# Zero-padded filter products, and a later inverse transform, in a one-core encoder trunk

## The chip, the cores and the metric

The program runs on one core of a Trainium2 chip. A core has a matmul engine (TensorE, PE in the profile, with its weight loads listed as PEld), a vector engine (VectorE, DVE), a scalar engine (ScalarE, ACT), GpSimd (POOL) and SyncE (SP), which here issues nearly all weight transfers. Each engine works through its own queue in order; they wait for one another through semaphores. The metric is the device time of one execution in microseconds (us), lower is better. The kernel before took 1728.81 us, the median of three runs (1728.32, 1728.81, 1731.26).

## The reference, cut to what matters

Two layers. Each has a hybrid token mixer (a short gated convolution and a Hyena operator, merged by gates) and then a channel mixer: a dense SwiGLU in layer 0, a top-2-of-8 expert SwiGLU in layer 1. One sequence of 256 positions, 1024 channels, float32. The change touches the Hyena part: its filters come out of a small network, and they are applied by Fourier transforms over all positions.

```python
def implicit_filters(L, w1, b1, freq, w2, b2, w3):
    z, t = hyena_pos_features(L)
    h = jnp.sin(fr * (z @ w1 + b1))
    h = jnp.sin(fr * (h @ w2 + b2))
    h = (h @ w3).reshape(L, N_DIRECTIONS, D_HYENA)          # the filter product
    h = h * decay_window(t)[:, None, :]
    h = h * lax.rsqrt(jnp.sum(jnp.square(h), axis=0, keepdims=True) + 1e-6)
    return h[:, 0], h[:, 1]

def bidirectional_fft_conv(u, k_fwd, k_bwd):
    kf = jnp.fft.rfft(kern, n=2 * L, axis=0)
    uf = jnp.fft.rfft(u, n=2 * L, axis=1)
    return jnp.fft.irfft(uf * kf[None], n=2 * L, axis=1)[:, :L]

    # in hybrid_mixer
    z = h_v * h_x1
    z = bidirectional_fft_conv(z, k_fwd, k_bwd) + z * hyena_bias
    y_h = h_x0 * z
    merged = g_a * (y_a @ w_a_out) + g_h * (y_h @ w_h_out)
    return merged @ w_o
```

## The kernel before, in words

**Number format.** TensorE multiplies in a reduced float32 form, so every operand is split into a high and a low part (`hilo`: ScalarE copies the high part, L167, VectorE subtracts it from the source, L168), and a product is made of three matmuls (`mm3`, L174 to L176). Weights arrive as chunks of 128x2048 floats (1 MB) in the buffers `wt`; each chunk is split in two halves, into six buffers `hl`, up to five halves ahead of their use.

**Chunks.** One projection of a 128x2048 weight chunk is 48 matmuls of 256 columns that accumulate into one of three PSUM banks called `mm`. In the mixer of either layer the order is: eight chunks for v and x1; then sixteen chunks, called here q0 to q15: four for x0, and twelve of the gated convolution, three for each quarter j. Of these three the first is copied out by ScalarE (L728), the second is multiplied by it on VectorE (L731, followed by the taps L583 and L585), the third is multiplied into the result by VectorE (L739) and split (`big`, L167 and L168). So q4, q7, q10 and q13 are of the first kind, q5, q8, q11 and q14 of the second, q6, q9, q12 and q15 of the third. Then come the sixteen chunks of the gate stage (per quarter: gate, `w_a_out`, gate, `w_h_out`), mixed with those of `w_o`. A bank `mm` is free again when the chunk three before has been taken out of it.

**The Fourier work** runs between the chunks, in two halves of the channels. `dft_a(half)` is 12 matmuls of 512 columns into four banks `acc`, and VectorE and ScalarE evict them (L660 to L662). `dft_b(half, q)` is the product with the filter's spectrum: four VectorE products (L672 to L675) and two on GpSimd (L676, L677). `dft_c(half)` is four GpSimd sums (L686, L687), each split into `yh` and `yl` by ScalarE and VectorE. `idft(half)` is the inverse transform: eight groups of four matmuls (L705 to L708), evicted by VectorE (L711, L714), multiplied by x0 on GpSimd (L717) and split. Its result is wanted by the first `w_h_out` chunk, the fourth chunk of the gate stage. Which of these steps follows which chunk stands in a table, `after`, which begins at chunk `o` and lists one entry per chunk:

```python
        o = 5 if l == 0 else 1
        for q, ev in enumerate(([(dft_a, 0)], [(dft_b, 0, 0)], [(dft_b, 0, 1)], [(dft_a, 1), (dft_c, 0)], [(dft_b, 1, 0)],
                                [(dft_b, 1, 1), (idft, 0)], [], [(dft_c, 1)], [], [(idft, 1)])):
```

So in layer 0 `dft_a(0)` follows q5 and `idft(1)` follows q14; in layer 1 they follow q1 and q10. The table gives the program order; a scheduler then sets the order of each engine's queue from it.

**The filters.** `flt_c(l, ct)`, eight for each layer, is a filter product: for each of two directions, one matmul of the network's output `fr` (128 rows: the high part of the 64 hidden units, twice) with the weights `wr` (64 rows high part, 64 rows low part), L405, and one of `fl` (64 rows: the low part) with the upper half of `wr`, L406. Layer 0's filters run between its own chunks (into banks `acc`); those of layer 1 run in layer 0's gate stage (four), between layer 0's mixer and its FFN (two) and in the FFN (two), into banks `mm`.

**Later stages.** After layer 1's mixer all the mixer's buffers become weight buffers (`W.extend`), and the expert stage streams its weights through them. Already in layer 1's gate stage three of the large buffers `big` are turned into weight buffers; SyncE fills them as soon as what used them is done.

Of the kernel before, what the change touches and what calls it, by code (L numbers as in the profile page):

```python
# [9 lines left out]
F32 = mybir.dt.float32  # L10
F32R = mybir.dt.float32r
BF16 = mybir.dt.bfloat16
I32 = mybir.dt.int32
U32 = mybir.dt.uint32
AF = mybir.ActivationFunctionType
ALU = mybir.AluOpType

P = 128
S = 256
# [194 lines left out]
def body(tc, nc, x, vec, rows, fg, winT, zT, fw1, fw2, fb, fw3, w_in, w_ao, w_ho, w_o, w13, w2,  # L214
         m13, m2, cst, out, dbg=None):
# [36 lines left out]
    xp = mix.enter_context(tc.tile_pool(name="xp", bufs=1))  # L252
    tmp = mix.enter_context(tc.tile_pool(name="tmp", bufs=10))

    def big8(shape, dt=F32):
        t = big.tile(list(shape), dt, name="big", tag="big")
        return t

    def t2k(shape=(P, 2, 256), dt=F32):
        t = tmp.tile(list(shape), dt, name="t2k", tag="t2k")  # L260
        return t
# [72 lines left out]
    W.load(3)  # L334
    ff = xp.tile([P, 2, 4, P], F32R)
    gg = xp.tile([P, 4, 2, P], F32R)
    fg_raw = big8([P, 2, 4, P])
    nc.sync.dma_start(fg_raw, fg)


    def sin_of(ps, l):

        b, which, n = ps[1], ps[2], ps[3]
        a = t2k([n, 256])
        nc.vector.tensor_scalar(out=a, in0=ps[0], scalar1=fb_s[:n, l, which:which + 1],
                                scalar2=fb_s[:n, l, 1:2], op0=ALU.add, op1=ALU.mult)
        q = t2k([n, 256])
        nc.vector.tensor_scalar(out=q, in0=a, scalar1=1.0 / TWO_PI, scalar2=MAGIC, op0=ALU.mult, op1=ALU.add)
        nc.vector.tensor_scalar(out=q, in0=q, scalar1=-MAGIC, scalar2=None, op0=ALU.add)
        for c in (C1, C2, C3):  # L350
            nc.vector.scalar_tensor_tensor(out=a, in0=q, scalar=-c, in1=a, op0=ALU.mult, op1=ALU.add)
        last["sin"] = nc.vector.tensor_scalar(out=a, in0=a, scalar1=-PI_F, scalar2=PI_F, op0=ALU.max, op1=ALU.min)
        last["sina"] = nc.scalar.activation(b, a, AF.Sin)
# [3 lines left out]
    def flt_bank(l, shape=(P, 2, 256)):  # L357
        return acc_bank(shape) if l == 0 else mm_bank(shape)

    def flt_h(l, which):  # L360

        n = 64 * (1 + which)
        if which == 0:
            flt_load(l, 0)
            flt_load(l, 1)
            lhs, rhs = fw1_s[:, l], zT_s
        else:
            lhs, rhs = fw2_s[:, l], fs.pop((l, "h"))
        ps = flt_bank(l, [n, S])
        nc.tensor.matmul(ps, lhs, rhs, start=True, stop=True)  # L370
        t = xp.tile([n, S], F32, name="fh", tag="fh")
        sin_of((ps, t, 2 * which, n), l)
        if which == 0:
            fs[l, "h"] = t
        else:
            fs[l] = xp.tile([P, S], F32R, name="fr", tag="fr"), xp.tile([64, S], F32R, name="fl", tag="fl")
            nc.scalar.activation(fs[l][0], t, AF.Copy)
            nc.vector.tensor_tensor(out=fs[l][1], in0=t[:64], in1=fs[l][0][:64].bitcast(F32), op=ALU.subtract)

    def flt_load(l, ct):  # L380
        if ct < 8:
            wn = tmp.tile([P, S], F32, name="wn", tag="wn", bufs=3)
            nc.sync.dma_start(wn, winT[ct])
            w3 = tmp.tile([P, 2, P], F32, name="w3", tag="w3", bufs=2)
            nc.sync.dma_start(w3, fw3[l, ct])
            fs[l, "w", ct] = wn, w3

    def flt_w(l, ct):

        if (l, "w", ct) in fs:  # L390
            wn, w3 = fs.pop((l, "w", ct))
            wr = tmp.tile([P, 2, P], F32R, name="wr", tag="wr", bufs=2)
            with tc.issue_after(last["sina"].ins):
                nc.scalar.activation(wr, w3, AF.Copy)
            nc.vector.tensor_tensor(out=wr[64:], in0=w3[64:], in1=wr[64:].bitcast(F32), op=ALU.subtract)
            fs[l, "p", ct] = wn, wr
            flt_load(l, ct + 2)

    def flt_c(l, ct):

        flt_w(l, ct)
        wn, wr = fs.pop((l, "p", ct))
        ps = flt_bank(l)
        for s in range(2):
            nc.tensor.matmul(ps[:, s], wr[:, s], fs[l][0], start=True, stop=False)  # L405
            nc.tensor.matmul(ps[:, s], wr[:64, s], fs[l][1], start=False, stop=True)  # L406
        if ct != 4 or l == 0:
            flt_w(l, ct + 1)
        hw = t2k()
        nc.vector.tensor_tensor(out=hw, in0=ps, in1=wn[:, None, :].to_broadcast([P, 2, S]), op=ALU.mult)  # L410
        ss = small.tile([P, 2], F32, name="ss", tag="ss")
        sd = t2k()
        for s in range(2):
            nc.scalar.activation(sd[:, s], hw[:, s], AF.Square, accum_out=ss[:, s:s + 1])
        rn = small.tile([P, 2], F32, name="rn", tag="rn")
        nc.gpsimd.tensor_scalar(out=rn, in0=ss, scalar1=1e-6, scalar2=None, op0=ALU.add)
        nc.gpsimd.tensor_tensor(out=rn, in0=rn, in1=mhalf, op=ALU.pow)
        for s in range(2):
            nc.scalar.activation(hw[:, s], hw[:, s], AF.Copy, scale=rn[:, s:s + 1])
        nc.gpsimd.memset(hw[:, 1, 0:1], 0.0)  # L420
        for s, op in enumerate((ALU.add, ALU.subtract)):
            nc.gpsimd.tensor_tensor(out=sd[:, s], in0=hw[:, 0], in1=hw[:, 1], op=op)
        fs[l, "sd", ct] = sd
# [44 lines left out]
    fs = {}  # L468
# [104 lines left out]
    def proj(parts, xs):  # L573

        xh, xl = xs
        ps = mm_bank()
        for pt in range(2):
            for k in range(KT):
                mm3(nc, ps[:, pt], parts(pt * D + k * P, P), (xh(k), xl(k)), k == 0, k == KT - 1)
        return ps  # L580
# [20 lines left out]
    def mixer(l, xh, xl):  # L601
# [21 lines left out]
        for j in range(4):  # L623
            ps = proj(W.next(), xs)
# [7 lines left out]
            ps = proj(W.next(), xs)  # L632
# [111 lines left out]

        sts = [{} for _ in range(4)]
        chunks = [(x0_chunk, j) for j in range(4)] + [(a_chunk, j, w, sts[j]) for j, w in A_ORDER]
        o = 5 if l == 0 else 1
        after = {1: [(z_parts, 3)]}
        for q, ev in enumerate(([(dft_a, 0)], [(dft_b, 0, 0)], [(dft_b, 0, 1)], [(dft_a, 1), (dft_c, 0)], [(dft_b, 1, 0)],
                                [(dft_b, 1, 1), (idft, 0)], [], [(dft_c, 1)], [], [(idft, 1)])):  # L750
            after[o + q] = after.get(o + q, []) + ev
        for q, (f, *a) in enumerate(chunks):
            f(*a)
# [16 lines left out]
        if l == 0:  # L770
            with W.behind():
                nc.scalar.activation(tri_b, tri_s, AF.Copy)
            steps.extend([[(flt_h, 1, 0)], [], [(flt_h, 1, 1)], [], [(flt_c, 1, 0)], [(flt_c, 1, 1)]]
                         + [[(flt_t, 1, c - 2), (flt_c, 1, c)] for c in (2, 3)] + [[(flt_t, 1, 2)], [(flt_t, 1, 3), (flt_w, 1, 5)]])

        for j in range(4):
            ps = proj(W.next(), xs)
# [3 lines left out]
            ps = proj(W.next(), yas)  # L781
            nc.vector.tensor_tensor(out=ga, in0=ps, in1=ga, op=ALU.mult)
            fill0()
            ps = proj(W.next(), xs)
# [3 lines left out]
            ps = proj(W.next(), yhs)  # L788
# [54 lines left out]
    with W.behind():  # L843
        flt_h(0, 0)
    W.after = (last["sin"].ins,)
    steps.extend([[], [], [(flt_h, 0, 1)], [(flt_c, 0, 0)], [(flt_c, 0, 1)]])
    for c in range(2, 8):
        steps.append([(flt_t, 0, c - 2), (flt_c, 0, c)] + ([(flt_d, 0, c // 2 - 2)] if c in (4, 6) else []))
# [4 lines left out]
    li = 0  # L853
    for l in range(DEPTH):
        acc = mixer(l, xh, xl)
        li += 1
        if l == 1:
# [373 lines left out]
    for r, v in enumerate(nc.values_load_multi_w_load_instructions(ix[0:1], engines=[mybir.EngineType.SP], min_val=0,  # L1231
# [4 lines left out]
                            in1=keys[:, None, :].to_broadcast([P, NE, NE]), op=ALU.is_equal)  # L1236
# [155 lines left out]
```

## Time and profile before

| | |
|---|---|
| median of three runs | 1728.81 us |
| the profiled execution, whole | 1726.32 us |
| its span in the profile | 1724.4 us |
| PE busy (share of the span) | 1670.5 us (97%) |
| DVE busy | 710.5 us (41%) |
| ACT busy | 491.7 us (29%) |
| POOL busy | 180.3 us (10%) |
| mean granted clock of TensorE | 0.982 |

The shares are means over unlike stages. In the page's picture of 40 slices (43.1 us each) VectorE is at 80 to 90% in most of the slices that hold layer 0's mixer (the first six), at about half in the FFN, high again in layer 1's mixer, and at 10 to 20% in the expert stage, which is over half of the span and runs at 90% or more on PE and on the DMA engines. A busy PE is no measure of its speed, as matmuls overlap: the distance from one start to the next is, and that is read from the timeline. What it waits for is in the list of waits.

### The profile page before, as it was taken

The page shows a single profiled execution, that of the slowest core. Times are in us where ns is not written, and L with a number is a line of the kernel's source. Part 1 is how long each engine was busy: PE and PEld are TensorE (multiplying, and loading weights), DVE is VectorE, ACT ScalarE, POOL GpSimd, SP SyncE. Part 2 cuts the span into 40 slices and gives each one's busy share as a digit, 9 for nine tenths or more (in the row PEclk, how much of TensorE's full clock was granted, in tenths as well). Part 3 has the DMA queues.
Part 4 walks back from the last instruction along what each step waited for, and adds up shares of the span by engine and source line. Part 5 has one row for each costly group of instructions (what it writes and reads, how often), then busy time and mean ns, then how long its engine had stood idle before and what let it go on. Part 6 is the DMA issues. An engine that isn't in the chain of part 4 may idle for free. (4 is left out here: it accounts for less than half of the span.)

```text
span 1724.4 us, 32503 instructions
## 1 busy us (share of the span) xinstructions
PE 1670.5 (97%) x14105; PEld 1091.8 (63%) x14105; DVE 710.5 (41%) x1009; ACT 491.7 (29%) x775; POOL 180.3 (10%) x163
## 2 busy tenths in 40 slices
PE   7999899899998999999999999999999999999996
PEld 6999899799997999999534333343343333434322
DVE  8989865765557899655410110101101011010112
ACT  4763565454543554543110100000001010010110
POOL 3424311210102034000110000000000000000000
PEclk9999999999998999999999999999999999999998
DMA  7443355355452543656698999999999999999993
GB/s 280 161 165 120 144 192 208 122 176 193 173 195 100 194 147 142 250 174 245 248 396 347 399 419 419 420 418 418 368 415 419 419 419 419 373 367 373 418 420 135
DMA packets 73580, 491.91 MB, mean 285 GB/s; under 512 B 8278, under 2 KB 13144, under 8 KB 14808
## 3 DMA queue, kind: packets, MB, share of 16 engines
q1 hardware_dynamic: 73000, 486.63, 71.7%
q0 software_dynamic: 432, 3.15, 0.5%
q8 instruction: 112, 1.84, 0.4%
q14 instruction: 36, 0.29, 0.0%
HBM read 488.70 MB, written 1.05 MB: 284 GB/s over the span
## 5 line engine op out<-in xcount | busy, mean ns | idle before, releaser
L1047 PE MATMUL mm<-wt,xe 128*32 128x512 f32 (+1 forms) x3664 | 473.5, 542 | 0.0
L176 PE MATMUL mm<-xh,hl 128*128 128x256 f32 x1376 | 393.0, 286 | 5.9 <-DVE hl L168 5.9
L174 PE MATMUL mm<-xh,hl 128*128 128x256 f32 x1376 | 394.4, 287 | 2.0 <-ACT xh L167 1.1
L175 PE MATMUL mm<-xl,hl 128*128 128x256 f32 x1376 | 393.2, 286 | 2.9 <-DVE xl L168 2.7
L168 DVE TENSOR_TENSOR hl<-wt,hl 128x1024 fp32r<-128x1024 f32 x234 | 305.7, 1311 | 145.2 <-ACT hl L167 144.4
L1047 PE MATMUL mm<-big,xe 128*32 128x512 f32 (+1 forms) x1712 | 295.9, 535 | 0.0
L167 ACT ACTIVATE hl<-wt 128x1024 fp32r<-128x1024 f32 x234 | 245.1, 1054 | 172.5 <-PE mm L176 97.4
L1047 PEld LDWEIGHTS mm<-wt,xe 128*32 128x32 f32 x3664 | 155.7, 110 | 210.9 <-issue 189.9
L176 PEld LDWEIGHTS mm<-xh,hl 128*128 128x128 f32 x1376 | 267.4, 194 | 6.4 <-DVE hl L168 6.3
L174 PEld LDWEIGHTS mm<-xh,hl 128*128 128x128 f32 x1376 | 267.6, 195 | 5.4 <-ACT xh L167 1.9
L175 PEld LDWEIGHTS mm<-xl,hl 128*128 128x128 f32 x1376 | 267.1, 194 | 4.9 <-DVE xl L168 3.9
L1057 DVE TENSOR_TENSOR act<-mm,act 128x512 f32<-128x512 f32 (+1 forms) x32 | 20.0, 625 | 483.4 <-PE mm L1047 483.4
L1096 PE MATMUL acc<-wt,at 128*32 128x512 f32 x1232 | 192.8, 593 | 0.0
L1047 PEld LDWEIGHTS mm<-big,xe 128*32 128x32 f32 x1712 | 86.4, 110 | 101.9 <-issue 91.4
L1056 ACT ACTIVATE act<-mm 128x512 f32<-128x512 f32 (+1 forms) x32 | 17.4, 544 | 457.0 <-PE mm L1047 457.0
L490 POOL TENSOR_TENSOR rs<-rs,mhalf 128x1 f32<-128x1 f32 x10 | 6.8, 675 | 1076.9 <-DVE rs L489 1076.9
L1096 PEld LDWEIGHTS acc<-wt,at 128*32 128x32 f32 x1232 | 53.1, 110 | 83.7 <-issue 82.9
L1096 PE MATMUL acc<-big,at 128*32 128x512 f32 x544 | 101.3, 593 | 0.0
L1101 PE MATMUL acc<-wt,bt 128*32 128x512 f32 x352 | 100.2, 592 | 0.0
L174 PE MATMUL mm<-big,hl 128*128 128x256 f32 x256 | 72.5, 283 | 0.0
L176 PE MATMUL mm<-big,hl 128*128 128x256 f32 x256 | 72.3, 282 | 0.0
L175 PE MATMUL mm<-big,hl 128*128 128x256 f32 x256 | 72.2, 282 | 0.0
(249 smaller groups left out, 1811.3 us busy)
## 6 DMA issues: line engine op xcount, KB each, us to landing
wt<-in_m_dram SPq DMA_DIRECT2D x231, 1024.0 KB, 12.6
big<-in_m_dram SPq DMA_DIRECT2D x103, 1024.0 KB, 13.3
wt<-in_w_in_dram SPq DMA_DIRECT2D x62, 1024.0 KB, 4.8
wt<-in_w_dram SPq DMA_DIRECT2D x33, 1024.0 KB, 4.9
wt<-in_w_ho_dram SPq DMA_DIRECT2D x8, 1024.0 KB, 5.7
wt<-in_w_ao_dram SPq DMA_DIRECT2D x7, 1024.0 KB, 4.8
wt<-in_w_o_dram SPq DMA_DIRECT2D x6, 1024.0 KB, 4.9
big<-in_rows_dram POOLq DMA_DIRECT2D x3, 1024.0 KB, 7.7
```

The lines of the kernel that those rows point to most:

```text
L167: a = nc.scalar.activation(hi, src, AF.Copy)
L168: v = nc.vector.tensor_tensor(out=lo, in0=src, in1=hi.bitcast(F32), op=ALU.subtract)
L174: nc.tensor.matmul(out, ah, bh, start=start, stop=False)
L175: nc.tensor.matmul(out, ah, bl, start=False, stop=False)
L176: nc.tensor.matmul(out, al, bh, start=False, stop=stop)
L490: last["pow"] = nc.gpsimd.tensor_tensor(out=rs, in0=rs, in1=mhalf[:, 0:1], op=ALU.pow)
L1047: nc.tensor.matmul(banks[r][32 * q:32 * q + 32, :n], xe[:, k, 32 * sg:32 * sg + 32], cols(w, b, q4), start=k == 0, stop=k == KT - 1, tile_ ...
L1056: nc.scalar.activation(a[:, :n], banks[0][:, :n], AF.Silu)
L1057: nc.vector.tensor_tensor(out=a[:, :n], in0=banks[1][:, :n], in1=a[:, :n], op=ALU.mult)
L1096: nc.tensor.matmul(ya[32 * q:32 * q + 32], at[:, f, 64 * b + 32 * sg:64 * b + 32 * sg + 32], ch[b][0][:, h * D + db * 512:h * D + (db + 1) ...
L1101: nc.tensor.matmul(yb[32 * q:32 * q + 32], bt[:, f, 32 * b:32 * b + 32], ch[b][0][:, h * D + db * 512:h * D + (db + 1) * 512], start=first ...
```

## The change

The low part `fl` is now one tile of 128 rows, made once and shared by both layers; its lower 64 rows are set to zero at the start by VectorE, and the second matmul of a filter product takes all 128 rows of `wr`. In the table, layer 0 begins one chunk earlier, and `idft(1)` stands two entries further back: in layer 0 all Fourier steps but `idft(1)` come one chunk earlier, and `idft(1)` one chunk later, after q15; in layer 1 `idft(1)` comes two chunks later, after q12, and nothing else moves.

```diff
+    fl = xp.tile([P, S], F32R)
+    nc.vector.memset(fl[64:].bitcast(U32), 0)
...
-            fs[l] = xp.tile([P, S], F32R, name="fr", tag="fr"), xp.tile([64, S], F32R, name="fl", tag="fl")
+            fs[l] = xp.tile([P, S], F32R, name="fr", tag="fr"), fl
             nc.scalar.activation(fs[l][0], t, AF.Copy)
-            nc.vector.tensor_tensor(out=fs[l][1], in0=t[:64], in1=fs[l][0][:64].bitcast(F32), op=ALU.subtract)
+            nc.vector.tensor_tensor(out=fl[:64], in0=t[:64], in1=fs[l][0][:64].bitcast(F32), op=ALU.subtract)
...
             nc.tensor.matmul(ps[:, s], wr[:, s], fs[l][0], start=True, stop=False)
-            nc.tensor.matmul(ps[:, s], wr[:64, s], fs[l][1], start=False, stop=True)
+            nc.tensor.matmul(ps[:, s], wr[:, s], fs[l][1], start=False, stop=True)
...
-        o = 5 if l == 0 else 1
+        o = 4 if l == 0 else 1
...
-                                [(dft_b, 1, 1), (idft, 0)], [], [(dft_c, 1)], [], [(idft, 1)])):
+                                [(dft_b, 1, 1), (idft, 0)], [], [(dft_c, 1)], [], [], [], [(idft, 1)])):
```

Lines after the new tile have a number higher by three in the changed kernel (L739 is L742 there). The scheduler's order moves with the table. VectorE's queue in layer 0, around q5 (whose product is L731): before, the eviction of `dft_a(0)` (L661, L662) stands behind that of q5 and of the last filter step (L460, L461).

```order
L168 TENSOR_TENSOR big<-acc,big 128x4x128
L168 TENSOR_TENSOR hl<-wt,hl 128x1024 x2
L731 TENSOR_TENSOR t2k<-mm,t2k 128x512
L168 TENSOR_TENSOR hl<-wt,hl 128x1024
L583 SCALAR_TENSOR_TENSOR t2k<-t2k,vec_s 128x255 x2
L585 SCALAR_TENSOR_TENSOR t2k<-t2k,vec_s 128x255 x2
L460 TENSOR_TENSOR big<-acc,t2k 128x256
L461 TENSOR_TENSOR big<-t2k,acc 128x256
L460 TENSOR_TENSOR big<-acc,t2k 128x256
L461 TENSOR_TENSOR big<-t2k,acc 128x256
L661 TENSOR_TENSOR t2k<-acc,t2k 128x512 x2
L662 TENSOR_TENSOR t2k<-t2k,acc 128x512 x2
```

Now, the same place of the same queue:

```order
L168 TENSOR_TENSOR big<-acc,big 128x4x128
L168 TENSOR_TENSOR hl<-wt,hl 128x1024
L664 TENSOR_TENSOR t2k<-acc,t2k 128x512 x2
L665 TENSOR_TENSOR t2k<-t2k,acc 128x512 x2
L168 TENSOR_TENSOR hl<-wt,hl 128x1024
L734 TENSOR_TENSOR t2k<-mm,t2k 128x512
L168 TENSOR_TENSOR hl<-wt,hl 128x1024
```

The eviction of `dft_a(0)` has moved ahead of q5's and of one weight split. VectorE's queue in layer 0 between the eviction of q11 (L731) and what follows that of q12 (L739), before:

```order
L731 TENSOR_TENSOR t2k<-mm,t2k 128x512
L168 TENSOR_TENSOR hl<-wt,hl 128x1024
L583 SCALAR_TENSOR_TENSOR t2k<-t2k,vec_s 128x255 x2
L585 SCALAR_TENSOR_TENSOR t2k<-t2k,vec_s 128x255 x2
L168 TENSOR_TENSOR hl<-wt,hl 128x1024
L739 TENSOR_TENSOR t2k<-mm,t2k 128x512
L168 TENSOR_TENSOR hl<-wt,hl 128x1024
L168 TENSOR_TENSOR big<-t2k,big 128x512 x5
```

And now:

```order
L734 TENSOR_TENSOR t2k<-mm,t2k 128x512
L168 TENSOR_TENSOR hl<-wt,hl 128x1024
L586 SCALAR_TENSOR_TENSOR t2k<-t2k,vec_s 128x255 x2
L588 SCALAR_TENSOR_TENSOR t2k<-t2k,vec_s 128x255 x2
L168 TENSOR_TENSOR big<-t2k,big 128x512 x4
L168 TENSOR_TENSOR hl<-wt,hl 128x1024
L742 TENSOR_TENSOR t2k<-mm,t2k 128x512
L168 TENSOR_TENSOR hl<-wt,hl 128x1024
```

The four splits of `dft_c(1)`, which `idft(1)` reads, have moved ahead of q12's eviction; the fifth `big` is q12's own. VectorE's queue in layer 1 from the eviction of q9 (L739) on, before; L711 and L714 are evictions of `idft(1)`, L731 that of q11:

```order
L739 TENSOR_TENSOR t2k<-mm,t2k 128x512
L168 TENSOR_TENSOR hl<-wt,hl 128x1024
L168 TENSOR_TENSOR big<-t2k,big 128x512
L168 TENSOR_TENSOR hl<-wt,hl 128x1024
L711 SCALAR_TENSOR_TENSOR t2k<-big,vec_s,acc 128x2x128
L168 TENSOR_TENSOR hl<-wt,hl 128x1024
L714 TENSOR_TENSOR t2k<-acc,t2k 128x2x128
```

And now:

```order
L742 TENSOR_TENSOR t2k<-mm,t2k 128x512
L168 TENSOR_TENSOR hl<-wt,hl 128x1024
L168 TENSOR_TENSOR big<-t2k,big 128x512
L168 TENSOR_TENSOR hl<-wt,hl 128x1024 x3
L734 TENSOR_TENSOR t2k<-mm,t2k 128x512
L168 TENSOR_TENSOR hl<-wt,hl 128x1024
L586 SCALAR_TENSOR_TENSOR t2k<-t2k,vec_s 128x255 x2
L588 SCALAR_TENSOR_TENSOR t2k<-t2k,vec_s 128x255 x2
```

Up to the third row the two queues are the same; behind it the evictions of `idft(1)` have gone back behind those of q11 and q12. Over the whole program VectorE's queue holds one instruction more than before, the zeroing; the other engines have the same instructions, and GpSimd also the same order.

## Rows read from the trace of the kernel before

**Rows 1.** Timeline, PE, one filter product (start us, duration us, engine, line, operation).

```profile
63.03 0.36 PE L405 MATMUL acc<-fr,wr 128*128 128x256 f32 x1
63.33 0.38 PE L406 MATMUL acc<-fl,wr 64*128 64x256 f32 x1
...
64.49 0.28 PE L175 MATMUL mm<-xl,hl 128*128 128x256 f32 x1
```

**Rows 2.** Timeline, PE, layer 0 from q14 to the gate stage (idle before, releaser).

```profile
183.30 0.36 PE L174 MATMUL mm<-xh,hl 128*128 128x256 f32 x1 [0.95 <-DVE t2k L731]
...
189.00 0.28 PE L176 MATMUL mm<-xh,hl 128*128 128x256 f32 x1
191.46 0.38 PE L705 MATMUL acc<-gg,big 128*128 128x256 f32 x1 [2.18 <-ACT big L167]
...
200.06 0.28 PE L174 MATMUL mm<-xh,hl 128*128 128x256 f32 x1
...
205.81 0.28 PE L174 MATMUL mm<-xh,hl 128*128 128x256 f32 x1
```

**Rows 3.** Timeline, PE, layer 1 from the end of q10 to q13.

```profile
674.91 0.28 PE L176 MATMUL mm<-xh,hl 128*128 128x256 f32 x1
675.88 0.39 PE L705 MATMUL acc<-gg,big 128*128 128x256 f32 x1 [0.69 <-ACT big L167]
...
684.83 0.28 PE L705 MATMUL acc<-gg,big 128*128 128x256 f32 x1
...
685.29 0.28 PE L174 MATMUL mm<-xh,hl 128*128 128x256 f32 x1
...
696.79 0.28 PE L174 MATMUL mm<-xh,hl 128*128 128x256 f32 x1
```

**Rows 4.** Stretches: length; busy us (instructions) by engine; PEclk, DMA share, GB/s.

```profile
57.00:121.00 64.00, 64.00 (x495) 60.77 (x496) 54.50 (x88) 46.55 (x104) 28.29 (x42) 1.00 0.49 166
121.31:190.16 68.85, 67.02 (x535) 65.44 (x533) 65.11 (x79) 27.12 (x38) 30.25 (x18) 1.00 0.35 123
192.90:199.70 6.80, 5.94 (x28) 5.94 (x29) 6.80 (x9) 5.25 (x8) 0.00 (x0) 0.50 0.58 226
677.60:684.40 6.80, 5.44 (x24) 5.25 (x25) 6.80 (x9) 4.26 (x6) 0.00 (x0) 0.50 0.42 157
840.00:860.00 20.00, 20.00 (x179) 9.34 (x180) 7.12 (x46) 2.10 (x4) 0.92 (x2) 1.00 0.20 67
860.00:1700.00 840.00, 831.97 (x7954) 317.48 (x7946) 82.79 (x146) 71.96 (x137) 5.52 (x2) 1.00 0.97 399
```

**Rows 5.** Tile fl: matmuls, duration ns min/median/max, first and last start.

```profile
L406 PE MATMUL acc<-fl,wr x16: 379/382/382, 54.8 to 105.2; 64*128 64x256 f32 x16
...
L406 PE MATMUL mm<-fl,wr x16: 379/382/579, 242.1 to 467.2; 64*128 64x256 f32 x16
```

**Rows 6.** Timeline, PEld, layer 0's second filter product.

```profile
55.88 0.19 PEld L405 LDWEIGHTS acc<-fr,wr 128*128 128x128 f32 x1 [0.24 <-DVE wr L395]
```

**Rows 7.** Timeline, PE, the first FFN chunk of layer 0.

```profile
343.44 0.41 PE L174 MATMUL mm<-xh,hl 128*128 128x256 f32 x1
343.98 0.58 PE L175 MATMUL mm<-xl,hl 128*128 128x256 f32 x1
```

**Rows 8.** Timeline, DVE: start of the program; layer 0; layer 1.

```profile
3.44 0.69 DVE L485 BATCH_NORM_STATS2 st<-big 128x6 f32<-128x512 f32 x1 [2.43 <-DMA big<-in_x_dram]
...
191.22 3.09 DVE L168 TENSOR_TENSOR big<-t2k,big 128x512 fp32r<-128x512 f32 x5
...
207.80 0.69 DVE L168 TENSOR_TENSOR big<-t2k,big 128x512 fp32r<-128x512 f32 x1 [2.13 <-ACT big L167]
...
681.04 0.68 DVE L739 TENSOR_TENSOR t2k<-mm,t2k 128x512 f32<-128x512 f32 x1
```

**Rows 9.** Timeline, POOL and SP, layer 1: last of idft(1), and a large buffer's transfer.

```profile
690.68 1.29 POOL L717 TENSOR_TENSOR t2k<-t2k,big 128x512 f32<-128x512 f32 x1 [1.87 <-DVE t2k L714]
...
706.00 0.38 SPq L99 DMA_DIRECT2D big<-in_w_ao_dram  x1
```

## The prediction

> **What bounds the kernel now.** I read the list of TensorE's waits first, then its timeline where it waits, then VectorE's queue beside it, and the stretches last. Two places stand out, one in each layer, and they are the same step: `idft(1)`. In layer 0 its first matmul starts at 191.46, 2.18 us of idling after q14's last one, and the step reaches to 200.06 [rows 2]; in layer 1 it reaches from 674.91 + 0.12 to 685.29 [rows 3]. Without a halt the eight groups take 8 x 0.46 = 3.7 us, by the last group of layer 1 (684.83 to 685.29) [rows 3]. Two things stretch it. It waits for the high and low parts of `dft_c(1)`, which stand late in the queues of ScalarE and VectorE. And right after these waits the granted clock is 0.50 for 6.8 us, in both layers [rows 4]: 1.2 GHz instead of 2.4, so the rest of the step runs at half speed. The third place is smaller but comes often: the filter products. Four of their matmuls and the one behind them take 63.03 to 64.49 = 1.46 us [rows 1], while a chunk's matmuls of the same 256 columns follow each other at (205.81 - 200.06) / 48 = 0.12 us [rows 2]. Every step into or out of a 64-row matmul costs 0.3 us from start to start; durations do not show this, because matmuls overlap.
>
> Behind TensorE stands VectorE. From 121.31 to 190.16 it is busy 65.11 of 68.85 us [rows 4]. So what TensorE is spared in layer 0 must be checked against VectorE's queue, not only against its own.
>
> The expert stage, more than half of the span, runs its DMA engines at a share of 0.97 [rows 4]. It passes an earlier start on in full, by this reading: between 840 and 860 the share is 0.20, since all buffers are already full, so the stream is tied to the buffers that the mixer's end hands over, and these come earlier by what the mixer saves.
>
> **The filter products.** Five starts at 0.12 instead of 1.46 us save 1.46 - 0.60 = 0.86 us a product, if 128 rows throughout remove the 0.3 us steps. There are 16 products (32 matmuls with `fl`, two each) [rows 5]. Not all lie on TensorE's path. Layer 0's first is followed at once by the second, which waits for its weights until 55.88 [rows 6], so the first gives nothing. The two between mixer and FFN are followed by a chunk that has to halt at its fifth start or so for the low part of the input (a step of 0.54 us at 343.98 where the half clock's step is 0.21) [rows 7]; they give nothing either. That leaves 7 in layer 0's chunks, 4 in the gate stage and 2 in the FFN. In the last two places TensorE waits for nobody, and I take the saving in full: 4 x 0.86 = 3.4 and 2 x 0.86 = 1.7 us.
>
> In layer 0 the seven are worth 6.0 us to TensorE. VectorE must follow; from 57 to 121 it is busy 54.50 of 64 us [rows 4], so it has 9.5 us of idle time, most of it spent waiting for ScalarE, whose work here follows TensorE's. I take 5.0 of the 6.0 us; the ends are 0 and 6.0. A loss is excluded, since 128-row matmuls cost 0.12 us everywhere else. The zeroing at the start costs nothing: VectorE idles 2.43 us there until x lands [rows 8]; without that cover it would be under 0.7 us, the row next to it.
>
> The Trainium skill speaks against all of this: its page TensorE: Matmul & The Clock Gate (Why this matters for your kernels) holds that one matmul on few rows takes the same time as one on 128, so that 64 more rows change nothing; by it this part is worth 0. Another page of the Trainium skill, TensorEngine Tiling (Array Packing), Key Properties, says that a change of tiling mode drains the engine; by it the part is worth what I have set. The trace leans to the second: 0.30 us from L405 to L406 [rows 1].
>
> **`idft(1)` in layer 1.** Nothing before q10's end moves, so the old times hold up to there: 675.03. Now q11 follows at once and ends at 675.03 + 5.75 = 680.8. q12 needs the bank of q9, which VectorE takes out at 681.04 + 0.68 = 681.7 [rows 8]; its queue is the same up to there, so q12 begins at 681.8, 1.0 us late, and ends at 687.5. By then the parts of `dft_c(1)` are long split, since the old step was through by 685.29. `idft(1)` takes 3.7 us without a halt, and q13 starts at 691.2 instead of 696.79 [rows 3]: 5.6 us. The ends are 685.29 - 675.03 - 3.7 = 6.6 (no wait at q12) and 3 (a halt for the second half's weights or a slower clock behind the wait). Halts of 0.95 us are no cause for the half clock here: after that at 183.30 in layer 0 the 48 matmuls took 189.12 - 183.30 = 5.8 us [rows 2].
>
> What is queued behind `idft(1)` moves with it. GpSimd's last product of it ends now at 690.68 + 1.29 = 692.0, and SyncE fills the third of the freed large buffers at 706.00 [rows 9]. Moved to 691.2 + 7 = 698, that product still ends before 706.00, so the weight queue is not held up.
>
> **The table in layer 0.** TensorE by itself would be spared the 0.95 us before q14 and the excess of `idft(1)`, 200.06 - 189.12 - 3.7 = 7.2: 8.2 us. VectorE gives less. The last thing that q15 waits for is the eviction of q12 (L739, L742 now), as q15 takes q12's bank. In the old order that eviction ends at 190.16, and from 121.31 to there VectorE has 65.11 us of work [rows 4]. The new order has the same instructions in front of it and, as the second pair of queue pieces shows, four splits more: 4/5 of 3.09 = 2.5 us [rows 8]. Run without a gap that is 121.31 + 67.6 = 188.9; with some 0.4 us at the start for `dft_a(0)`'s copies, 189.3. Then q15 (5.75) and `idft(1)` (3.7), which finds its inputs split before q15 began: the gate stage starts at 198.7 instead of 205.81 [rows 2], 7.1 us. If VectorE comes 5.0 us earlier through the filter products, both add: 12.1 us. TensorE's own bound then is 8.2 + 6.0 = 14.2 us, so VectorE sets the pace. Ends: 14.2, and 3.7, where VectorE gains nothing and one more halt brings 6.8 us at half speed as above, which costs 3.4 us. The result of `idft(1)` is late by nothing: before, its last split ends at 208.5 [rows 8], 8.4 us after the step; the first `w_h_out` chunk comes three chunks, 17 us, after it. Some 4 us more of queue stand before those evictions now, and it still fits.
>
> **The sum**, against the profiled execution of 1726.3 us: 7.1 + 5.0 + 3.4 + 1.7 + 5.6 = 22.8, so 1703.5. That execution lies 2.5 us under the median of the runs, which I add: 1706.0 us, or 1.3% faster.
>
> **Rivals.**
>
> *Rows do not matter.* The 0.3 us steps come from something else than 64 rows, such as one bank written twice in a row, and stay. For it: the two matmuls of a pair do share bank and weights. Against: the three matmuls of every split product share a bank too, and follow at 0.12. Then the filter terms go and the table's stay: 7.1 + 5.6 = 12.7, so 1716.1 us.
>
> *VectorE takes it back.* In layer 0 it is full, the earlier Fourier steps only push it into saturation sooner, it does not come forward at all, and TensorE's halts gather into one that again brings the half clock: 3.7 instead of 12.1 us, in all 14.4, so 1714.4 us. For it: 65.11 of 68.85 us. Against: 9.5 idle us ahead of that stretch.
>
> *Half clock for a long stretch, slower.* From q8 to q15 of layer 0 TensorE now waits a little at each chunk for VectorE, and the clock does not come back between. Each chunk then costs 5.75 us more; from five such chunks on the gain is eaten and the kernel is slower, and all eight would give about 1706 + 46 = 1752 us. For it: both halts before brought 0.50. Against: it came back after 6.8 us each time, and by the walk above TensorE halts once, at q15, for 1 to 2 us.
>
> *The weight stream does not start earlier.* If the expert stage is timed by something that the mixer does not move, the end stays at 1728.8 us. Against: the 0.20 between 840 and 860.
>
> **How the numbers follow.** Chances: the forecast 0.74, rows do not matter 0.09, VectorE takes it back 0.11, the long half clock 0.03, the stream 0.03. The low end is everything at its best: 14.2 + 3.4 + 1.7 + 6.6 and 1.6 for the two products between the stages, 27.5, so 1701.3; the runs shown scatter by 2 to 3 us, so 1699. The upper end has to hold the first two rivals, 1714.4 and 1716.1, and the same scatter: 1719. A measurement can tell about 0.2% (3.5 us) from no change. The first three cases are faster by more than that: 0.94; the stream rival is the same, 0.03; the long half clock slower, 0.03.
>
> **What would show it.** Right: the filter products' matmuls 0.12 us apart; no wait in front of `idft(1)` in either layer, its groups at 0.46, no stretch at 0.50 there; q13 of layer 1 some 16.2 us after q10's end (21.8 now); in layer 0 one halt at q15 for L742 and the gate stage 12 us earlier; every later stage shifted by the sum. Wrong: steps of 0.3 us that stay, VectorE idle while TensorE waits for it, new rows at clock 0.50 between 120 and 200, or an expert stage that has grown by what the mixer saved.

## The result, and the profile after

The changed kernel takes 1709.27 us (median of 4 runs, 1708.96 to 1710.34) against 1728.62 us before (4 runs, 1728.32 to 1731.26): a ratio of 0.9886, 95% interval 0.9869 to 0.9903, or 19.4 us less. Forecast were 1706.0 us in a range of 1699 to 1719. The profiled execution took 1709.39 us, its span is 1707.6; between the two profiled executions lie 16.9 us, where 22.8 were forecast.

The filter products first: the timeline of TensorE in the changed kernel, one product (start us, duration us, engine, line), beside [rows 1]. The last two rows are the first two matmuls of the chunk behind it.

```profile
63.88 0.36 PE L408 MATMUL acc<-fr,wr 128*128 128x256 f32 x1
64.08 0.28 PE L409 MATMUL acc<-fl,wr 128*128 128x256 f32 x1
64.20 0.28 PE L408 MATMUL acc<-fr,wr 128*128 128x256 f32 x1
64.32 0.28 PE L409 MATMUL acc<-fl,wr 128*128 128x256 f32 x1
64.44 0.28 PE L174 MATMUL mm<-xh,hl 128*128 128x256 f32 x1
64.56 0.28 PE L175 MATMUL mm<-xl,hl 128*128 128x256 f32 x1
```

In the kernel before, the chunk's first matmul, which [rows 1] leaves out, is this one:

```profile
64.27 0.39 PE L174 MATMUL mm<-xh,hl 128*128 128x256 f32 x1
```

From the product's first start to the chunk's second matmul it is now 0.68 us, and was 1.46 (63.03 to 64.49); to the chunk's first matmul it is 0.56, and was 1.24. So the prediction's 1.46 us reaches one matmul further than "the one behind them". The wide steps are gone. Only behind the first matmul is there still a step of 0.20.

The same timeline in layer 0 from the end of q14 to the gate stage, beside [rows 2] (in brackets the idle time before and what ended it):

```profile
188.19 0.28 PE L176 MATMUL mm<-xh,hl 128*128 128x256 f32 x1
189.85 0.36 PE L174 MATMUL mm<-xh,hl 128*128 128x256 f32 x1 [1.38 <-DVE t2k L742]
...
195.68 0.28 PE L708 MATMUL acc<-gg,big 128*128 128x256 f32 x1
...
199.33 0.28 PE L174 MATMUL mm<-xh,hl 128*128 128x256 f32 x1
```

q15 now comes first and halts once, for VectorE's eviction of q12 (L742). `idft(1)` then runs without a halt from 195.68 to 199.33, 3.65 us instead of 8.6. The gate stage starts at 199.33 instead of 205.81: 6.48 us, where 12.1 were forecast.

Layer 1, beside [rows 3]:

```profile
669.19 0.28 PE L176 MATMUL mm<-xh,hl 128*128 128x256 f32 x1
670.40 0.36 PE L174 MATMUL mm<-xh,hl 128*128 128x256 f32 x1 [0.93 <-DVE t2k L742]
...
676.22 0.28 PE L708 MATMUL acc<-gg,big 128*128 128x256 f32 x1
...
679.88 0.28 PE L174 MATMUL mm<-xh,hl 128*128 128x256 f32 x1
```

The halt of about 1 us at q12 and the 3.66 us of `idft(1)` are what was forecast. The stretches, beside [rows 4] (length; busy us and instructions of PE, PEld, DVE, ACT, POOL; granted clock, DMA share, GB/s), show both steps at the upper clock level, 1.00 where 0.50 stood before. VectorE is as full as before (65.50 of 69 us from 121 to 190, a row shown with the experiments below). The expert stage passes the lead on: its transfer share is 0.98, and TensorE's lead is 16.9 us at layer 1's gate stage (697.15 against 714.07) and 16.8 in the span, so the rival in which the weight stream does not start earlier is out.

```profile
193.00:199.30 6.30, 6.30 (x56) 6.30 (x55) 6.30 (x9) 4.71 (x7) 0.00 (x0) 1.00 0.92 336
676.10:679.80 3.70, 3.70 (x35) 3.70 (x34) 3.70 (x7) 2.81 (x4) 0.00 (x0) 1.00 0.89 328
860.00:1680.00 820.00, 811.73 (x7770) 313.04 (x7766) 80.98 (x143) 70.24 (x134) 5.52 (x2) 1.00 0.98 400
```

TensorE's waits in the changed kernel from 110 to 206 us (total us, times, longest) show where layer 0 lost: the four waits of before (4.8 us) have gone, and 4.2 us of others have come, all for VectorE.

```profile
PE mm L176 <- DVE hl L168: 1.5, 2, 1.3
PE mm L174 <- DVE t2k L742: 1.4, 1, 1.4
PE acc L174 <- DVE big L168: 1.1, 2, 0.7
PE acc L174 <- DVE big L464: 0.2, 1, 0.2
```

### The profile page after: what moved, and what is told of

Its sections match the earlier page's. It is cut to its first block, busy times and chain, and to the rows that moved or that the text cites. A ratio compares the mean times of both kernels' runs of the same rounds, so it can differ in the third digit from the quotient of the medians.

```text
span 1707.6 us, 32515 instructions
## 1 busy us (share of the span) xinstructions
PE 1654.1 (97%) x14105; PEld 1084.6 (64%) x14105; DVE 707.9 (41%) x1010; ACT 489.8 (29%) x775; POOL 186.7 (11%) x163
## 3 DMA queue, kind: packets, MB, share of 16 engines
q0 software_dynamic: 432, 3.15, 0.5%
## 5 line engine op out<-in xcount | busy, mean ns | idle before, releaser
L1059 ACT ACTIVATE act<-mm 128x512 f32<-128x512 f32 (+1 forms) x32 | 17.4, 544 | 457.0 <-PE mm L1050 457.0
```

The lines of the kernel that those rows point to most:

```text
L1059: nc.scalar.activation(a[:, :n], banks[0][:, :n], AF.Silu)
```

## The experiments

The kernels reach this stretch up to 1.9 us apart at the same work, two profiles of the change 1.0 us. So for each profile I read a lead over the kernel before: how much earlier a TensorE chunk starts, less the difference at the chunk ahead of the filter products. That chunk's first matmul, before and in the changed kernel:

```profile
53.74 0.28 PE L174 MATMUL mm<-xh,hl 128*128 128x256 f32 x1
```

```profile
54.72 0.28 PE L174 MATMUL mm<-xh,hl 128*128 128x256 f32 x1
```

In that measure the changed kernel leads by (205.81 - 53.74) - (199.33 - 54.72) = 7.46 us at layer 0's gate stage and by 17.90 at layer 1's. In a second profile of it (e8_after, below) these are 7.48 and 17.26.

| kernel | chunk ahead of the products | gate stage, layer 0 | lead there | lead at layer 1's gate stage | median us |
|---|---|---|---|---|---|
| before | 53.74 | 205.81 | 0 | 0 | 1728.62 |
| the change | 54.72 | 199.33 | 7.46 | 17.90 | 1709.27 |
| e1_filter | 54.21 | 200.69 | 5.59 | 9.71 | 1719.83 |
| e2_table | 54.59 | 201.90 | 4.76 | 9.11 | 1719.42 |
| e5_sums_dve | 54.16 | 195.56 | 10.67 | 20.29 | 1706.29 |
| e6_notaps | 55.54 | 197.00 | 10.61 | 20.49 | 1709.15 |
| e3_late_steps | 54.47 | 195.80 | 10.74 | 17.91 | 1711.25 |
| e7_late_sums | 54.85 | 193.68 | 13.24 | 22.70 | 1704.24 |
| e8_after | 53.68 | 198.27 | 7.48 | 17.26 | 1710.41 |

The medians come from three sets of runs, each with its own runs of the kernel before. That kernel took 1728.62 us beside the change, 1728.34 beside e1_filter, e2_table, e5_sums_dve and e6_notaps, and 1726.86 beside e3_late_steps, e7_late_sums and e8_after.

**The two parts alone.** The 128-row products with the old table:

```
...
-        fs[l] = ..., xp.tile([64, S], F32R, name="fl", tag="fl")
+        fs[l] = ..., fl
...
-            nc.tensor.matmul(ps[:, s], wr[:64, s], fs[l][1], ...)
+            nc.tensor.matmul(ps[:, s], wr[:, s], fs[l][1], ...)
```

> The 128-row filter products alone, with the old table. Theory (VectorE sets the pace through layer 0's chunks, so what TensorE is spared there is swallowed): the products' matmuls start 0.12 us apart, layer 0's gate stage starts at most 1 us earlier than the 205.81 us of before, and the gate stage (3.1 us), the FFN (1.6) and the step between them (0.6) give the rest: 5 to 6 us off the kernel before. Rival (VectorE follows TensorE, and it was the new table that cost the time again): the gate stage starts 4 to 5 us earlier, at 201 to 202, and the kernel is 9 to 10 us shorter.

And the table with the 64-row products:

```
-        o = 5 if l == 0 else 1
+        o = 4 if l == 0 else 1
-        ... [(dft_b, 1, 1), (idft, 0)], [], [(dft_c, 1)], [], [(idft, 1)])):
+        ... [(dft_b, 1, 1), (idft, 0)], [], [(dft_c, 1)], [], [], [], [(idft, 1)])):
```

> The new table alone, with the 64-row filter products. Theory (VectorE sets the pace in layer 0): the gate stage of layer 0 starts at 199 to 200 us, as in the changed kernel, because the eviction of q12 stands behind the same VectorE work; with 5.4 us in layer 1 that is 11 to 13 us off the kernel before, and the two parts alone then add up to 0 to 2 us less than the change together. Rival (the two parts add, TensorE's 4.8 us of the filter products reach the gate stage): the gate stage starts at 203 to 205 us, and the kernel is 7 to 8 us shorter. In both, filter products keep steps of 0.30 us.

Measured: 0.9949 (0.9933 to 0.9966) and 0.9941 (0.9924 to 0.9957) of the kernel before, 1728.34 us in these runs: 8.5 and 8.9 us. My theory was wrong in both, and the rival came nearer. With the old table the lead of the filter products reaches layer 0's gate stage whole: 4.8 us at q4, 5.6 there. The table alone brings 4.8 there, not 6.5 to 7.1. Alone they bring 5.59 + 4.76 = 10.35 us, together 7.46: 2.9 us are lost where both act on the same chunks. Outside layer 0 nothing is lost: the table alone gives layer 1 8.26 - 2.81 = 5.45 us (from its second chunk to its gate stage), the change 16.92 - 11.49 = 5.43. The medians do not resolve this (8.5 + 8.9 = 17.4 beside the change's 19.4, or 16.5 in e8_after's runs); it is read from the traces, one of each kernel.

TensorE's waits from 110 to 206 us, the filter products alone:

```profile
PE acc L708 <- ACT big L167: 2.2, 1, 2.2
PE mm L174 <- DVE t2k L734: 0.9, 1, 0.9
PE acc L710 <- DVE big L168: 0.7, 1, 0.7
PE acc L709 <- DVE big L168: 0.5, 1, 0.5
```

The same with the table alone:

```profile
PE mm L176 <- DVE hl L168: 1.5, 2, 1.3
PE mm L174 <- DVE t2k L739: 1.4, 1, 1.4
```

The old table keeps the halt in front of `idft(1)`, and with it the half clock: the granted clock is 0.50 from 187.00 to 193.70 and from 668.30 to 675.00 in the first kernel.

```profile
187.00:193.70 6.70, 5.35 (x22) 4.87 (x23) 6.70 (x9) 5.88 (x9) 0.00 (x0) 0.50 0.56 177
668.30:675.00 6.70, 5.16 (x23) 4.98 (x24) 6.70 (x10) 4.16 (x6) 0.00 (x0) 0.50 0.41 153
```

The new table alone shows the same waits at `hl` and for q12's eviction (L739, L742 in the change), but not those at `acc`. Those are `dft_a(0)`, which now stands ahead of q5. TensorE reaches it 4.65 us sooner with the filter products (q4 starts at 109.49 against 114.14), before VectorE has taken out its banks. It halts 0.48 + 0.16 + 0.67 us, and q5 starts only 2.55 us sooner (120.63 against 123.18). From there to the gate stage the difference stays at 2.5 to 2.6: both kernels halt in the same places for the same time.

VectorE had not come forward with TensorE. Its weight split ahead of these evictions, with the table alone and then in the change:

```profile
118.58 1.22 DVE L168 TENSOR_TENSOR hl<-wt,hl 128x1024 fp32r<-128x1024 f32 x1
```

```profile
117.94 1.22 DVE L168 TENSOR_TENSOR hl<-wt,hl 128x1024 fp32r<-128x1024 f32 x1
```

That is 0.64 us sooner (0.77 as a lead), where TensorE is 4.65 sooner. With the old table it is the same up to there: the same split comes at 117.38 with the filter products and at 117.74 before, a lead of 0.83. But behind it VectorE's waits for the other engines shrink, and at the split that starts at 126.58 before, and at 122.25 with the filter products, its lead is 4.8. The new order asks VectorE for `dft_a(0)`'s banks before that.

In VectorE's timeline with the table alone the idle time that my walk had left out is to be seen:

```profile
127.34 1.23 DVE L168 TENSOR_TENSOR hl<-wt,hl 128x1024 fp32r<-128x1024 f32 x1 [1.56 <-ACT hl L167]
129.13 0.69 DVE L731 TENSOR_TENSOR t2k<-mm,t2k 128x512 f32<-128x512 f32 x1 [0.56 <-PE mm L176]
130.22 1.23 DVE L168 TENSOR_TENSOR hl<-wt,hl 128x1024 fp32r<-128x1024 f32 x1 [0.40 <-ACT hl L167]
...
173.73 0.69 DVE L168 TENSOR_TENSOR big<-t2k,big 128x512 fp32r<-128x512 f32 x1 [1.03 <-ACT big L167]
...
191.58 0.68 DVE L739 TENSOR_TENSOR t2k<-mm,t2k 128x512 f32<-128x512 f32 x1
```

These are 3.55 us in which VectorE waits for ScalarE or TensorE, although it is the fullest engine; q12's eviction ends at 192.26, not at 190.2 (the walk's 189.3 and 0.85 us of later start).

**Is it VectorE?** Two kernels relieve it behind q5. One leaves TensorE's work alone and takes some 5 us from VectorE; it leaves out the taps of the convolution in layer 0's second branch:

```
                     nc.scalar.activation(o[:, pt], c[:, pt], AF.Copy, scale=vcol(wb, 3 * pt + 1))
-                    conv_taps(o, c, wb, pt)
+                    if l:
+                        conv_taps(o, c, wb, pt)
```

> The changed kernel without the taps of the gated convolution in layer 0's second branch, which leaves out part of the computation and takes about 5 us from VectorE between q5 and q15; TensorE's work is the same. Theory (VectorE sets the pace): q15's wait of 1.38 us for the eviction of q12 goes, and layer 0's gate stage starts 2.5 to 3.5 us earlier than 199.33, as much as TensorE waits for VectorE from q9 on. Rival (TensorE or ScalarE sets it): the gate stage starts at most 0.5 us earlier.

The wait at q15 is gone and the lead at the gate stage is 10.61, 3.15 us more than the change's: as the theory had it, in this measure (197.00 against 199.33 is 2.33). Its median, 1709.15 us, shows none of that: in its profile 0.6 us are lost in the expert stage, 1.5 at the last normalization (VectorE waits 2.7 us there, 1.1 in the changed kernel), and it began 0.8 later.

The other gives VectorE more instructions and takes them from GpSimd, because VectorE's instructions are longer beside GpSimd's:

```
-            nc.gpsimd.tensor_tensor(out=a, in0=a, in1=b, op=ALU.subtract)
-            nc.gpsimd.tensor_tensor(out=xr, in0=xr, in1=xi, op=ALU.add)
+            nc.vector.tensor_tensor(out=a, in0=a, in1=b, op=ALU.subtract)
+            nc.vector.tensor_tensor(out=xr, in0=xr, in1=xi, op=ALU.add)
```

and the same for the two sums of `dft_c`.

> The changed kernel, with the sums and differences of dft_b and dft_c (16 a layer) on VectorE instead of GpSimd. Theory (VectorE loses about 0.95 us on each instruction that runs beside a GpSimd one, 13.8 us between 119 and 190 us): VectorE gets some 10 us of work more and loses most of those 13.8, so layer 0's gate stage starts 1 to 3 us earlier than 199.33, TensorE's waits there shrink, and the kernel is 1 to 4 us faster than the changed one. Rival (VectorE's long instructions are long for another reason): VectorE simply has 10 us more to do in each layer, the gate stage of layer 0 starts 5 to 9 us later, and the kernel is 5 to 15 us slower than the changed one.

Measured: 1706.29 us (1705.22 to 1707.62), ratio to before 0.9869 (0.9853 to 0.9886), against 0.9886 (0.9869 to 0.9903) and 0.9902 (0.9886 to 0.9919) for the change. These intervals overlap and the change was not run in that set, so the medians alone do not show the gain; the pair of e3_late_steps and e7_late_sums, below, does. The lead at the gate stage is 10.67 us, 3.2 more. Two stretches of the same 69 us, first the changed kernel, then this one (columns as above):

```profile
121.00:190.00 69.00, 66.09 (x536) 64.80 (x535) 65.50 (x82) 28.25 (x41) 35.94 (x18) 1.00 0.34 123
```

```profile
121.00:190.00 69.00, 68.52 (x562) 67.77 (x561) 65.45 (x101) 33.55 (x46) 2.59 (x2) 1.00 0.37 131
```

VectorE does 101 instructions instead of 82 in the same busy time, and TensorE 562 matmuls instead of 536. The groups of VectorE's instructions from 126.5 to 189 us by shape (count; busy us, mean ns of one; idle before), in the changed kernel:

```profile
L168 DVE TENSOR_TENSOR hl<-wt,hl 128x1024 fp32r<-128x1024 f32 x14 | 22.7, 1642 | 0.4 <-ACT hl L167 0.4
L676 DVE TENSOR_TENSOR t2k<-t2k,big 128x512 f32<-128x512 f32 x4 | 4.9, 1230 | 0.0
```

and with the sums on VectorE:

```profile
L168 DVE TENSOR_TENSOR hl<-wt,hl 128x1024 fp32r<-128x1024 f32 x17 | 20.4, 1216 | 0.4 <-ACT hl L167 0.4
L676 DVE TENSOR_TENSOR t2k<-t2k,big 128x512 f32<-128x512 f32 x4 | 2.7, 683 | 0.0
```

The long instructions had been waiting for GpSimd inside their own duration: 1642 ns became 1216, 1230 became 683. Those that read one input from a bank are not stretched. In the changed kernel's timeline, VectorE first and then GpSimd, two splits of weights take 4.55 us beside GpSimd's sums, and the two of L664, which read `acc` while the second sum runs, 1.28, as long as the same two take at 123.30 with the table alone, where GpSimd idles:

```profile
142.72 4.55 DVE L168 TENSOR_TENSOR hl<-wt,hl 128x1024 fp32r<-128x1024 f32 x2
147.19 1.28 DVE L664 TENSOR_TENSOR t2k<-acc,t2k 128x512 f32<-128x512 f32 x2
```

```profile
144.03 2.16 POOL L689 TENSOR_TENSOR t2k<-t2k 128x512 f32<-128x512 f32 x1
146.27 2.17 POOL L690 TENSOR_TENSOR t2k<-t2k 128x512 f32<-128x512 f32 x1
```

The relieved kernels reach the same lead, 10.6 to 10.7, with the same waits left: 1.3 us at `dft_a(0)`, which lies ahead of what they relieve, and 0.5 at `hl`. Otherwise TensorE's own work sets the pace there.

**The place of the Fourier steps.** The change with layer 0's earlier steps put back, `idft(1)` still behind q15:

```
-        o = 4 if l == 0 else 1
+        o = 5 if l == 0 else 1
-        ... [(dft_c, 1)], [], [], [], [(idft, 1)])):
+        ... [(dft_c, 1)], []) + (([], [(idft, 1)]) if l == 0 else ([], [], [(idft, 1)]))):
```

> The changed kernel, but layer 0's Fourier steps up to dft_c(1) stay one chunk later, where the kernel before had them; idft(1) still comes after q15 there, and layer 1 is as in the changed kernel. Theory (the filter products' gain reaches VectorE whole in the old order, and the new one loses it twice: TensorE halts before and in dft_a(0) ahead of q5, and the splits of dft_c(1) now stand ahead of q12's eviction): no halt at q5, q15 waits at most 1.2 us, idft(1) does not wait because its inputs are split by 190 us; the gate stage of layer 0 starts some 10.8 us earlier than before, counted from the first filter product, instead of 7.5, and the kernel is 2.5 to 3.5 us faster than the changed one. Rival (VectorE has that much work in either order): the gate stage starts within 1 us of the changed kernel's, and the two are equal.

The first half came as forecast: no halt at q5, 1.0 us at q15, no wait at `idft(1)`, and a lead of 10.74 at the gate stage (10.8 expected). But the time did not: 1711.25 us beside 1710.41 for the change on the same chip. Within the gate stage the lead falls to 7.3 again. First a row of TensorE's timeline, then VectorE's ahead of the same moment:

```profile
209.96 0.39 PE L174 MATMUL mm<-xh,hl 128*128 128x256 f32 x1 [1.72 <-DVE t2k L348]
```

```profile
204.12 0.69 DVE L168 TENSOR_TENSOR big<-t2k,big 128x512 fp32r<-128x512 f32 x1 [0.90 <-ACT big L167]
...
207.28 0.69 DVE L168 TENSOR_TENSOR big<-t2k,big 128x512 fp32r<-128x512 f32 x1 [2.13 <-ACT big L167]
...
209.37 0.53 DVE L348 TENSOR_SCALAR t2k<-mm,fb_s 64x256 f32<-64x256 f32 x1
```

VectorE has the same queue to work off, then waits 0.90 and 2.13 us for the parts of `idft(1)`'s result, and behind these waits stands L348, the eviction of layer 1's filter, for whose bank TensorE now halts. Behind this halt the granted clock is 0.50 from 211.10 to 214.30. The halt was moved, not removed.

**Both reliefs together**, the late steps and the sums on VectorE:

> The late Fourier steps of layer 0 and the sums of dft_b and dft_c on VectorE, together. Theory (with VectorE relieved and no halt at q5, TensorE alone sets the pace of layer 0's chunks): no halt over 0.6 us between q5 and the gate stage, which starts 12 to 13.5 us earlier than before, counted from the first filter product; the kernel is 4 to 6 us faster than the changed one, and 1 to 3 us faster than with the sums on VectorE alone. Rival (TensorE's bound was reached with the sums alone, at 10.7 us): the gate stage starts at 10.7 again, and the time is that of the sums alone.

Measured: 1704.24 us (1703.12 to 1706.46), ratio to before 0.987 (0.9854 to 0.9887), 6.2 us under the change on the same chip, and its slowest run (1706.46) is under the change's fastest there (1708.89): a version that beats both kernels. It differs from the late steps alone (1711.25, ratio 0.9908, 0.9892 to 0.9925) only in the sums. Moving these to VectorE is worth 7.0 us there in the medians and 22.70 - 17.91 = 4.8 in the lead at layer 1's gate stage; the late steps' profile loses another 2.4 in the expert stage (see the last run). The profile lists no wait of TensorE between 115 and 206 us any more, the lead at the gate stage is 13.24, and of it 13.1 is left three chunks on.

**The price of a step between row counts**, in the kernel before, with the second pair of a product in the other order:

```
-        for s in range(2):
-            nc.tensor.matmul(ps[:, s], wr[:, s], fs[l][0], start=True, stop=False)
-            nc.tensor.matmul(ps[:, s], wr[:64, s], fs[l][1], start=False, stop=True)
+        nc.tensor.matmul(ps[:, 0], wr[:, 0], fs[l][0], start=True, stop=False)
+        nc.tensor.matmul(ps[:, 0], wr[:64, 0], fs[l][1], start=False, stop=True)
+        nc.tensor.matmul(ps[:, 1], wr[:64, 1], fs[l][1], start=True, stop=False)
+        nc.tensor.matmul(ps[:, 1], wr[:, 1], fs[l][0], start=False, stop=True)
```

> The kernel before, with its 64-row filter products kept, but the second pair of each product in the other order: 128, 64, 64, 128 rows instead of 128, 64, 128, 64. Theory (a step between row counts costs, not the row count): only two of a product's five starts are 0.30 us apart and the others 0.12, so a product takes 0.85 to 0.9 us instead of 1.23 and layer 0's q4 chunk starts 2.3 to 2.7 us earlier. Rival (each 64-row matmul costs, or a second write to the same bank does): the product still takes 1.2 us, whatever stands beside it, and nothing moves.

Measured: 1724.36 us against 1726.86, ratio 0.9981 (0.9972 to 0.9991). One product in TensorE's timeline:

```profile
63.87 0.36 PE L404 MATMUL acc<-fr,wr 128*128 128x256 f32 x1
64.16 0.38 PE L405 MATMUL acc<-fl,wr 64*128 64x256 f32 x1
64.38 0.28 PE L406 MATMUL acc<-fl,wr 64*128 64x256 f32 x1
64.59 0.39 PE L407 MATMUL acc<-fr,wr 128*128 128x256 f32 x1
64.81 0.28 PE L174 MATMUL mm<-xh,hl 128*128 128x256 f32 x1
64.93 0.28 PE L175 MATMUL mm<-xl,hl 128*128 128x256 f32 x1
```

From the first start to the chunk's second matmul: 1.06 us with two changes of the row count, 1.46 with four [rows 1], 0.68 with none. That is 0.19 to 0.20 us a change, and the count of 64-row matmuls is the same in the first two. q4 starts 2.5 us earlier (2.3 to 2.7 expected). The expected pattern did not show: the starts are 0.29, 0.22, 0.21, 0.22 and 0.12 apart, so the sum follows the number of changes, while its single steps do not.

**The change again**, beside these on one chip:

> The changed kernel unchanged, beside the others on the same chip, as their measure. Expected within 0.1% of its first time, 1709 us.

1710.41 us, against 1726.86 for the kernel before. Its profile lost 2.1 us near 1040 us, where TensorE waits for the expert stage's weights:

```profile
PE mm L1050 <- DMA wt<-in_m_dram: 1.4, 2, 0.9
```

The first profile of the change has no such wait. The table alone, the late steps and the reordered product lost 2.2 to 2.6 us at the same place.

## Why the prediction was right, and where its sizes were off

*The mechanisms* came as described: no wider steps, no halt and no half clock at `idft(1)` in either layer, a halt at q15 for L742, an expert stage that passes the lead on. Not forecast were the halts ahead of q15, 1.3 us at `dft_a(0)` and 1.5 at `hl`. Rows do not matter, the first rival, is refuted by the 128-row products alone and by the reordered product. The Trainium skill's page TensorE: Matmul & The Clock Gate (Why this matters for your kernels) says that few rows take the time of 128. The recorded durations agree (0.28 us for the 64-row matmul at 64.38 behind another one, as for that of 128 rows at 64.08 in the change), the starts do not: two changes of the row count lengthen a product by 0.38 us. A drain, of which the Trainium skill's page TensorEngine Tiling (Array Packing), Key Properties, speaks without a figure, would fit these 0.2 us a change; no row here shows the drain itself. The long half clock did not come.

*The step that was mis-sized* is "If VectorE comes 5.0 us earlier through the filter products, both add: 12.1 us". It measured 7.46 (6.48 without the correction for the start). Of this the table is 4.76 rather than 7.1: the walk ran VectorE's queue without a gap, and it has gaps of 3.55 us, much as in the old order, whose 68.85 - 65.11 = 3.74 idle us [rows 4] the walk dropped. The filter products add 2.7 rather than 5.0. The 5.0 came from VectorE's 9.5 idle us ahead of 121, said to wait mostly for ScalarE, "whose work here follows TensorE's". It did not follow: in either order VectorE was only 0.8 us further ahead at its last splits before 119. One of its waits there, at 111.50 in the change, is 1.89 us for ScalarE, which had waited 1.63 us for GpSimd's part of the last filter's norm (L420); both waits are as long with the 64-row products. So TensorE alone ran ahead, by 4.8 us at q4, and what came of that hung on the order. With the old table VectorE caught up behind q5; that the 5.0 then fits the 5.59 is luck, since they were not gained in that idle time. The new order puts `dft_a(0)` in front of q5, where TensorE comes too early for VectorE. The forecast had that rival, *VectorE takes it back*, at 3.7 with the half clock; it came about by half, without it. That VectorE sets the pace behind q5 was right for the change: both reliefs bring 3.2 us. But the late steps reach the same lead at the gate stage by the order alone, and pay for it in the next three chunks.

*The other terms*: gate stage 3.10 (3.4 forecast, 9.58 - 6.48), FFN 1.55 (1.7), layer 1 5.43 (5.6). The four saved 0.78 rather than 0.86 us a product: two went from 1.46 to 0.68, as a step of 0.20 stays behind the first matmul, the other two from 1.37 to 0.59. The two products between mixer and FFN gave nothing in the end, as forecast: the lead is 11.19 where the FFN's first chunk begins (342.00 against 330.81) and 9.29 at the second. At the two passages between stages +0.36 us came about. The start took 0.98 us; in e8_after it is -0.06, so that is no effect of the change. In all 7.46 + 3.10 + 1.55 + 5.43 + 0.36 - 0.98 = 16.9.

*From profile to median*: I added 2.5 us because the profile of before lies that far under its median. The profile of after lies 0.1 above its own. Halts for weights near 1040 us, as in e8_after, are of that size and come in some executions only; that they account for before's 2.5 us was not shown, since its one profile has none. So some 2.5 of the 19.4 us between the medians come from no term of the sum, and that the forecast lies 3.3 us off in the median rather than 5.9 is luck. Beside e8_after the medians lie 16.5 us apart.

*Open*: what makes the weights late in some executions, and what holds VectorE back between 57 and 118 us, where one wait was followed to GpSimd and no run tried it. Of the 2.1 us that the lead loses at `dft_a(0)`, the list of waits has 1.3. The rest is no other cause: the list counts idle time from the end of the matmul before, and from start to start the three halts are 0.73, 0.33 and 0.84 us longer than with the table alone.

## What to carry to other kernels

Two savings on one stretch add only as far as the second-fullest engine follows; idle time of that engine is not free to use until it is known what it waits for. A walk through its queue must keep the gaps in which it waits for others. Before counting on a full VectorE, compare the mean duration of the same instruction with and without GpSimd work beside it: moving work to the full engine was a gain here (22.70 against 17.91 us of lead with the late steps). And follow a moved step to the next wait in the same queue; a lead of 10.7 us at the start of a stage was 7.3 three chunks later.

## What the runs showed of the hardware

- VectorE's instructions with both inputs in SBUF are stretched by GpSimd's tensor operations beside them (1230 instead of 683 ns, 1642 instead of 1216); those that read a bank are not (the two of L664: 1.28 us beside GpSimd). The Trainium skill's page SBUF — State Buffer, Who interferes with whom, says just this: two SBUF inputs contend with a GpSimd instruction that reads SBUF. I had read these durations as VectorE's own work.
- A change between 64-row and 128-row matmuls costs 0.19 to 0.20 us here, read over a whole product with none, two and four of them.
